# Half of the first modulation's weights streamed by TensorE, another order of the opening, and chunk 1's first products taken row tile by row tile

## The chip, the cores and the metric

The kernel runs on one core of a Trainium2 chip. The metric is device time of one execution in microseconds. The kernel before was run three times: median 1368.39 us, 1365.68 to 1372.27. A further execution was recorded by the hardware profiler; all rows of the profile are from that one.

The engines are named as in the profile: PE is TensorE (products), PEld its weight loads, DVE is VectorE, ACT is ScalarE, POOL is GpSimd, SP is SyncE, which issues nearly all loads and stores here.

## The reference

Two layers of a transformer trunk on 1024 tokens of width 1024 (batch 1), in float32. Each layer is

```
mod = silu(c) @ w_ada[layer] + b_ada[layer]          # 1024 -> 3 x 1024: shift, scale, gate
h   = rmsnorm(x, g_pre) * (1 + scale) + shift
y   = mixer(h)                                       # h @ w_in, attention of two kinds, gates, @ w_out
x   = x + gate * rmsnorm(y, g_post)
```

Layer 0's mixer is latent attention beside sliding-window attention; layer 1's is differential attention beside forgetting attention. The case is about the very beginning: layer 0's shift and scale (2048 numbers, each a sum over 1024 rows of `w_ada`), the first `h`, and the first columns of `h @ w_in`.

## The kernel before, in words

**Layout.** Everything is held transposed: a tile has 128 features as partitions and C = 512 tokens as columns. The 1024 tokens are two chunks, 0 and 1; the 1024 features are eight row tiles, kc 0 to 7. `x` is 8 tiles per chunk, 256 KB each.

**Products.** A value is held as a high part and a low part, both in the fp32r type, so that a product of a weight tile and a tile of h is three matmuls of 128x512 (`kstep`, lines 127, 128, 130): high x high, high x low, low x high. Eight row tiles are accumulated in one PSUM bank: 24 matmuls for 128 output features of one chunk. A weight is loaded in two halves of 256 KB through the ring `wr` (3 buffers, `weight`, line 107), and split: ACT copies the high part (line 91), POOL subtracts (line 92).

**The modulation.** `ada` takes four tiles of 128 outputs at a time, a *group*. The weights of a group come as eight tiles of 128x512 (rows kc, 512 outputs), `raw` with ten buffers. ACT scales the first by silu(c) (line 286), DVE multiplies and adds the other seven to the sum `acc` (line 283). Then the 128 partitions of `acc` have to be added up: `mod_tiles` does that with one plain f32 matmul of each 128 columns against a column of ones (line 295), and a few small DVE instructions add the bias and form shift and scale (lines 304, 306). Layer 0's shift and scale are four such groups; group q holds what the row tiles 2q and 2q + 1 of h need.

**The rms.** `squares` squares the eight tiles of x on ACT (line 190) and adds them on DVE (line 194). `rstd` sums over partitions with f32 matmuls (line 204), takes the inverse root with a dozen small DVE instructions, and spreads the result with f32 matmuls (line 219); ACT copies it out of PSUM (line 367).

**A tile of h.** `pre_norm`: DVE multiplies x by scale and rms (line 326). For even kc ACT makes the high part (line 332) and DVE the low one (line 333); for odd kc ACT adds the shift (line 329) and makes the high part (line 91), POOL the low one (line 92).

**The opening.** `run` walks through a string, `PLAN`, one letter a step: `x` and `y` load x of chunk 0 and chunk 1; `r` and `s` compute their rms; `A` is a modulation group; `W` loads and splits a weight and takes a PSUM bank; `n` makes tiles of h of chunk 0, as many as there are groups for; `m` makes two of chunk 1; `P` issues the products that have become possible with chunk 0, weight by weight. There are five weights (K = 5): three tiles of the latent query, two of the latent key and value. Their banks are the two halves of the pair S, then pj, o, pj. After the plan the five banks are emptied (`keep`: ACT lines 672 and 673, DVE line 674), and chunk 1's products follow, one weight after the other with all eight row tiles, in banks taken in the same order. Then `setup2`, and the remaining first-stage weights with the other modulation groups behind them (`ada_behind`, `project`).

**What sets the order.** The code is written in that order, but a list scheduler places the instructions: it takes what is ready by its own estimate of times, in the order of the code as priority, with `high_priority(offset=60)` moving the folds and the tiles of h ahead. So a loader, or a product whose bank is still full, is passed by a later one. The result is one fixed order for each engine; on the chip each engine takes its own in order and waits where something isn't there yet. SP likewise issues its loads in one order and waits where a buffer isn't free.

Of the kernel before, what the change touches and what calls it, by code (L numbers as in the profile page):

```python
# [14 lines left out]
AF = mybir.ActivationFunctionType  # L15
ALU = mybir.AluOpType
# [6 lines left out]
C = 512  # L23
# [4 lines left out]

PLAN = "xAWWrnWyPAWnAPWnsAPnnmmmmP"


class Trunk:
# [253 lines left out]
        with self.tc.high_priority(offset=60):  # L288
            self.mod_tiles(l, tiles, a)

    def mod_tiles(self, l, tiles, a):
        nc = self.nc
        p = self.psum("pt")
        for j in range(len(tiles)):
            nc.tensor.matmul(p[:, j:j + 1], a[:, j * 128:j * 128 + 128], self.ones, start=True, stop=True)
        runs = []
        for j, t in enumerate(tiles):
            if runs and t == runs[-1][1] + runs[-1][2] and t % 8:
                runs[-1][2] += 1
            else:  # L300
                runs.append([j, t, 1])
        for j, t, n in runs:
            m = self.mod[l][:, t:t + n]
            nc.vector.tensor_tensor(out=m, in0=p[:, j:j + n], in1=self.v_bada[:, l * 24 + t:l * 24 + t + n], op=ALU.add)
            if t // 8 == 1:
                nc.vector.scalar_tensor_tensor(out=m, in0=m, scalar=1.0, in1=self.v_gpre[:, l * 8 + t - 8:l * 8 + t - 8 + n],
                                               op0=ALU.add, op1=ALU.mult)
            elif t // 8 == 2:
                g = self.v_gpost[:, l * 8 + t - 16:l * 8 + t - 16 + n]
                nc.vector.scalar_tensor_tensor(out=m, in0=m, scalar=0.5, in1=g, op0=ALU.mult, op1=ALU.mult)  # L310
# [851 lines left out]
    def run(self):  # L1162
# [3 lines left out]
        h = [[], []]  # L1166
# [3 lines left out]
        with self.tc.tile_pool(name="early", bufs=1) as early:  # L1170
# [13 lines left out]
            for step in PLAN:  # L1184
# [4 lines left out]
                    rs[ch] = self.copied(self.rstd(self.squares(xs[ch]), 1024))  # L1189
                elif step == "A":  # L1190
                    tiles = [2 * q, 2 * q + 1, 8 + 2 * q, 9 + 2 * q]
                    self.drain(self.ada(0, lambda kc: I["wadaa"][q, kc], tiles,
                                        self.t("acc", [128, C], bufs=2, pool=early), raw))
                    q += 1
                elif step == "W":
                    j = first[len(ws)]
                    ws.append(self.weight(j[0], 8, 128, early if len(ws) > 1 else None))
                    banks.append(self.bank(True) if len(banks) < 5 else self.psum("o"))
                    done.append(0)
                elif step == "n":  # L1200
                    with self.tc.high_priority(offset=60):
                        for kc in range(len(h[0]), min(8, 2 * q)):
                            h[0].append(self.pre_norm(0, kc, xs[0][kc], rs[0]))
                elif step == "m":
                    for kc in range(len(h[1]), min(8, len(h[1]) + 2, len(h[0]))):
                        h[1].append(self.pre_norm(0, kc, xs[1][kc], rs[1]))
                else:
                    for n, (w, p) in enumerate(zip(ws, banks)):
                        for kk in range(done[n], len(h[0])):
                            self.kstep(p, w, kk, h[0][kk], kk == 0, kk == 7)  # L1210
                        done[n] = len(h[0])
# [4 lines left out]
            late = [first[n][3][0][3](0, banks[n]) for n in range(K)]  # L1216
            for kc in range(len(h[1]), 8):
                h[1].append(self.pre_norm(0, kc, xs[1][kc], rs[1]))
            for n in range(K):
                p = self.bank(True)  # L1220
                for k in range(8):
                    self.kstep(p, ws[n], k, h[1][k], k == 0, k == 7)
                late.append(first[n][3][0][3](1, p))
            for f in late:
                if f:
                    f()
# [215 lines left out]
```

## Time and profile before

| | |
|---|---|
| median of 3 runs | 1368.39 us (1365.68 to 1372.27) |
| the profiled execution's own time | 1368.67 us |
| its span, first to last instruction | 1366.9 us |
| mean granted TensorE clock | 0.987 |
| PE busy | 1269.7 us, 93% |
| DVE busy | 912.3 us, 67% |
| ACT busy | 734.4 us, 54% |
| POOL busy | 352.5 us, 26% |
| first product of a weight with h | at 29.12 us |
| last product of the first five weights | starts at 108.78 us |

How to read the rows: a row of a group is line, engine, operation, output<-input by the program's names, partitions x elements of both, count | busy us, mean ns of one | idle time of the engine just before them and what ended it. A row of a timeline is start, duration, engine, line, operation, count, and in brackets the idle time before it with its releaser. The record of a matmul has a modelled end and overlaps the next; the distance from start to start is its pace. "raw<-in_wadaa_dram" are the loads of the first modulation's weights; `wx` are weights held in the opening's own memory, `wh` and `wl` those in the common one.

### The profile page before, as it was taken

The page shows a single profiled execution, that of the slowest core. Times are in us where ns is not written, and L with a number is a line of the kernel's source. Part 1 is how long each engine was busy: PE and PEld are TensorE (multiplying, and loading weights), DVE is VectorE, ACT ScalarE, POOL GpSimd, SP SyncE. Part 2 cuts the span into 40 slices and gives each one's busy share as a digit, 9 for nine tenths or more (in the row PEclk, how much of TensorE's full clock was granted, in tenths as well). Part 3 has the DMA queues.
Part 4 walks back from the last instruction along what each step waited for, and adds up shares of the span by engine and source line. Part 5 has one row for each costly group of instructions (what it writes and reads, how often), then busy time and mean ns, then how long its engine had stood idle before and what let it go on. Part 6 is the DMA issues. An engine that isn't in the chain of part 4 may idle for free.

```text
span 1366.9 us, 20727 instructions
## 1 busy us (share of the span) xinstructions
PE 1269.7 (93%) x6876; PEld 1055.4 (77%) x6876; DVE 912.3 (67%) x2058; ACT 734.4 (54%) x1515; POOL 352.5 (26%) x324
## 2 busy tenths in 40 slices
PE   2899999999999999999979999999999999999996
PEld 1678778888777777777757878787888888887896
DVE  6855757777668785787866776667646564656475
ACT  4253226555558577765545554447545455556542
POOL 2243421331233215300003322321222212233400
PEclk9999999999999999999999999999999999999998
DMA  8606685555354444373533222212112121233283
GB/s 284 249 19 210 194 277 189 170 161 178 109 158 138 156 124 138 103 231 123 176 92 104 70 59 66 49 56 76 52 38 78 54 78 55 85 117 103 78 270 121
DMA packets 103723, 173.85 MB, mean 127 GB/s; under 512 B 16304, under 2 KB 25520, under 8 KB 103616
## 3 DMA queue, kind: packets, MB, share of 16 engines
q1 hardware_dynamic: 99104, 169.91, 38.9%
q10 hardware_dynamic: 4512, 2.62, 0.6%
q8 instruction: 54, 0.88, 0.3%
q14 instruction: 53, 0.43, 0.1%
HBM read 129.36 MB, written 31.72 MB: 118 GB/s over the span
## 4 chain that ended last, share of the span: by engine, by line
PE 42%; DVE 12%; ACT 6%; issue 5%; DMA 5%; POOL 1%; SPq 1%; POOLq 0%; DVEq 0%; ACTq 0%
PE pj L127 8%; PE pj L128 8%; PE pj L130 8%; PE S L441 6%; PE pt L501 3%; PE o L511 2%; DVE pt_l L92 1%; DVE p L463 1%; DMA wr<-in_wout_dram 1%; PE o L510 1%; ACT wh L91 1%; PE S L127 1%; PE S L130 1%; PE S L128 1%; DMA t<-wd 1%
## 5 line engine op out<-in xcount | busy, mean ns | idle before, releaser
L127 PE MATMUL pj<-h,wh 128*128 128x512 f32 (+1 forms) x816 | 338.9, 416 | 1.5 <-ACT wh L91 1.5
L128 PE MATMUL pj<-h,wh 128*128 128x512 f32 (+1 forms) x816 | 322.2, 395 | 0.0
L130 PE MATMUL pj<-h,wl 128*128 128x512 f32 (+1 forms) x800 | 316.0, 395 | 2.2 <-DVE wl L92 2.2
L92 POOL TENSOR_TENSOR wl<-wr,wh 128x512 fp32r<-128x512 f32 x126 | 166.4, 1330 | 461.5 <-ACT wh L91 428.9
L466 ACT ACTIVATE p<-p,sm 128x128 f32<-128x128 f32 (+3 forms) x192 | 148.8, 775 | 146.8 <-DVE sm L463 143.0
L92 DVE TENSOR_TENSOR pt_l<-pt,pt_h 128x512 fp32r<-128x512 f32 (+1 forms) x232 | 146.9, 635 | 99.4 <-ACT pt_h L91 97.5
L441 PE MATMUL S<-qk,qk 96*128 96x512 f32 (+5 forms) x720 | 175.3, 344 | 20.6 <-DVE sm L463 11.4
L130 PEld LDWEIGHTS pj<-h,wl 128*128 128x128 f32 x800 | 151.0, 189 | 35.0 <-DVE wl L92 3.8
L91 ACT ACTIVATE pt_h<-pt 128x512 fp32r<-128x512 f32 (+1 forms) x232 | 127.6, 552 | 89.3 <-PE pt L501 87.5
L127 PEld LDWEIGHTS pj<-h,wh 128*128 128x128 f32 (+1 forms) x816 | 153.9, 189 | 20.3 <-ACT wh L91 2.3
L441 PEld LDWEIGHTS S<-qk,qk 128*128 128x128 f32 (+1 forms) x720 | 120.2, 188 | 63.2 <-DVE sm L463 25.5
L128 PEld LDWEIGHTS pj<-h,wh 128*128 128x128 f32 (+1 forms) x816 | 154.4, 189 | 17.1 <-DVE h L92 0.2
L91 ACT ACTIVATE wh<-wr 128x512 fp32r<-128x512 f32 x165 | 100.9, 622 | 115.4 <-PE S L128 38.6
L501 PE MATMUL pt<-ident,p 128*128 128x128 f32 x840 | 134.3, 274 | 3.1 <-DVE p L945 3.1
L501 PEld LDWEIGHTS pt<-ident,p 128*128 128x128 f32 x840 | 101.5, 140 | 26.1 <-DVE p L945 4.4
L463 DVE CUSTOM_DVE_ANT_0 p<-S,mask 128x640 f32<-128x640 f32 (+7 forms) x128 | 96.0, 750 | 35.0 <-PE S L441 34.1
L510 PE MATMUL o<-pt_h,v 128*128 128x256 f32 (+1 forms) x408 | 106.3, 279 | 2.1 <-ACT pt_h L91 1.7
L511 PE MATMUL o<-pt_l,v 128*128 128x256 f32 (+1 forms) x408 | 102.3, 285 | 5.6 <-DVE pt_l L92 5.3
L348 POOL TENSOR_TENSOR t<-t,rs 128x512 f32<-128x512 f32 x26 | 36.8, 1414 | 229.0 <-DMA t<-t 147.4
L511 PEld LDWEIGHTS o<-pt_l,v 128*128 128x128 f32 x408 | 77.2, 189 | 16.6 <-DVE pt_l L92 11.2
L510 PEld LDWEIGHTS o<-pt_h,v 128*128 128x128 f32 x408 | 77.0, 189 | 11.2 <-ACT pt_h L91 4.8
L127 PE MATMUL S<-h,wh 128*128 128x512 f32 (+1 forms) x144 | 57.5, 399 | 3.9 <-ACT h L332 2.7
(317 smaller groups left out, 2288.6 us busy)
## 6 DMA issues: line engine op xcount, KB each, us to landing
wr<-in_wod_dram SPq DMA_DIRECT2D x80, 256.0 KB
wr<-in_wout_dram SPq DMA_DIRECT2D x68, 256.0 KB
ad<-in_wadab_dram SPq DMA_DIRECT2D x41, 256.0 KB
wr<-in_wev_dram SPq DMA_DIRECT2D x38, 256.0 KB
raw<-in_wadaa_dram SPq DMA_DIRECT2D x32, 256.0 KB
ogd<-t SPq DMA_DIRECT2D x32, 256.0 KB
t<-t SPq DMA_DIRECT2D x106, 64.0 KB
t<-rd SPq DMA_DIRECT2D x48, 128.0 KB
```

Of the source, the lines that this page charges most:

```text
L91: nc.scalar.activation(hi, src, AF.Copy)
L92: (lo_eng or nc.vector).tensor_tensor(out=lo, in0=src, in1=hi.bitcast(F32), op=ALU.subtract)
L127: nc.tensor.matmul(p, w[0][:, k, :m], h[0], start=first, stop=False)
L128: nc.tensor.matmul(p, w[0][:, k, :m], h[1], start=False, stop=last and w[1] is None)
L130: nc.tensor.matmul(p, w[1][:, k, :m], h[0], start=False, stop=last)
L348: nc.gpsimd.tensor_tensor(out=s, in0=s, in1=self.rs[:, cs], op=ALU.mult)
L441: nc.tensor.matmul(dst, a, k[:, s], start=(n == 0), stop=n == len(q) - 1)
L463: nc.vector.tensor_tensor_reduce(out=P[:, s], in0=S[:, s], in1=a, scale=-scale, scalar=init, op0=ALU.add, op1=ALU.min, accum_out=nm)
L466: nc.scalar.activation(P[:, :n], P[:, :n], AF.Exp, bias=nm, scale=-1.0, accum_out=l)
L501: nc.tensor.transpose(pt[:, n * 128:n * 128 + 128], b, self.ident)
L510: nc.tensor.matmul(o[:, qcols], w, hi[:, cols], start=start, stop=False)
L511: nc.tensor.matmul(o[:, qcols], w, lo[:, cols], start=False, stop=stop)
```

## The change

Three things.

1. A new `ada_first` takes the place of `ada` in the opening. Of a group's eight weight tiles the first four go to PE: a plain f32 matmul with the column kc of silu(c) as weight (one column) and the weight tile as the moving operand (512 columns), accumulated in a one-partition slice of an `o` bank. ACT copies that row of 512 to memory. The other four go on as before: ACT scales kc 4, DVE adds kc 5, 6 and 7. `mod_tiles` then folds both: for each 128 outputs one matmul of the row (one partition) against a one, and one of `acc` against the column of ones, into the same PSUM column.

2. The plan is another: the rms of chunk 0 directly behind its load, the groups one step ahead of the tiles of h of the group before, the second and third weight behind the third group, chunk 1's load behind the fourth. An `n` makes exactly two tiles.

3. Chunk 1's products of the five weights are issued in two sets, three weights and then two; in a set each row tile of h goes through all weights before the next.

```diff
-PLAN = "xAWWrnWyPAWnAPWnsAPnnmmmmP"
+
+PLAN = "xrAWAnAWWPnAyWPnsWPnmmmmP"
...
-    def mod_tiles(self, l, tiles, a):
+    def ada_first(self, l, w, tiles, a, row, raw):
+
+        nc = self.nc
+        p = self.psum("o")[:1]
+        for kc in range(8):
+            r = raw()
+            nc.sync.dma_start(r, w(kc))
+            if kc < 4:
+                nc.tensor.matmul(p, self.sc[:, kc:kc + 1], r, start=kc == 0, stop=kc == 3)
+                if kc == 3:
+                    nc.scalar.activation(row, p, AF.Copy)
+            elif kc > 4:
+                nc.vector.scalar_tensor_tensor(out=a, in0=r, scalar=self.sc[:, kc:kc + 1], in1=a,
+                                               op0=ALU.mult, op1=ALU.add)
+            else:
+                nc.scalar.activation(a, r, AF.Copy, scale=self.sc[:, kc:kc + 1])
+        with self.tc.high_priority(offset=60):
+            self.mod_tiles(l, tiles, a, row)
+
+    def mod_tiles(self, l, tiles, a, row=None):
         nc = self.nc
         p = self.psum("pt")
         for j in range(len(tiles)):
-            nc.tensor.matmul(p[:, j:j + 1], a[:, j * 128:j * 128 + 128], self.ones, start=True, stop=True)
+            s = slice(j * 128, j * 128 + 128)
+            if row is not None:
+                nc.tensor.matmul(p[:, j:j + 1], row[:, s], self.ones[:1], start=True, stop=False)
+            nc.tensor.matmul(p[:, j:j + 1], a[:, s], self.ones, start=row is None, stop=True)
...
                 elif step == "A":
                     tiles = [2 * q, 2 * q + 1, 8 + 2 * q, 9 + 2 * q]
-                    self.drain(self.ada(0, lambda kc: I["wadaa"][q, kc], tiles,
-                                        self.t("acc", [128, C], bufs=2, pool=early), raw))
+                    self.ada_first(0, lambda kc: I["wadaa"][q, kc], tiles, self.t("acc", [128, C], bufs=2, pool=early),
+                                   self.t("row", [1, C], bufs=2, pool=early), raw)
                     q += 1
...
-                        for kc in range(len(h[0]), min(8, 2 * q)):
+                        for kc in range(len(h[0]), len(h[0]) + 2):
                             h[0].append(self.pre_norm(0, kc, xs[0][kc], rs[0]))
...
-            for n in range(K):
-                p = self.bank(True)
+            for group in ((0, 1, 2), (3, 4)):
+                banks = {n: self.bank(True) for n in group}
                 for k in range(8):
-                    self.kstep(p, ws[n], k, h[1][k], k == 0, k == 7)
-                late.append(first[n][3][0][3](1, p))
+                    for n in group:
+                        self.kstep(banks[n], ws[n], k, h[1][k], k == 0, k == 7)
+                for n in group:
+                    late.append(first[n][3][0][3](1, banks[n]))
```

## The prediction

> **What bounds the kernel now.** I read the page first: TensorE (PE) is busy for 93% of the span, so time is mostly to be had where it isn't. The row of 40 slices puts the largest hole at the start, which is also where the whole change lies. So I cut the start into stretches (columns: stretch and its length, then busy us with counts of PE, weight loads, DVE, ACT and POOL, the granted clock, DMA share, GB/s).
>
> ```profile
> 0.00:10.40 10.40, 0.00 (x0) 0.00 (x0) 3.20 (x10) 4.83 (x8) 0.20 (x4) 1.00 0.74 242
> 10.40:29.10 18.70, 5.62 (x24) 5.26 (x24) 12.30 (x28) 7.91 (x13) 6.42 (x5) 1.00 0.81 278
> 29.10:56.00 26.90, 18.69 (x56) 13.86 (x56) 24.44 (x28) 11.71 (x19) 11.42 (x8) 0.87 0.78 278
> 56.00:85.30 29.30, 26.51 (x124) 20.09 (x124) 24.07 (x44) 14.82 (x25) 9.09 (x6) 1.00 0.28 105
> 85.30:109.00 23.70, 23.70 (x102) 19.21 (x103) 5.26 (x7) 9.54 (x18) 11.82 (x10) 1.00 0.13 39
> 109.00:160.00 51.00, 50.17 (x258) 41.90 (x257) 34.66 (x88) 12.99 (x25) 19.52 (x16) 1.00 0.69 216
> ```
>
> From 85.3 to 109.0 PE is full: 102 products in 23.7 us, 0.232 us each. Before that VectorE (DVE) is the full one, 24.4 of 26.9 us and 24.1 of 29.3. The timeline gives the chain.
>
> ```profile
> 13.33 5.47 DVE L283 SCALAR_TENSOR_TENSOR acc<-raw,sc,acc 128x512 f32<-128x512 f32 x7
> 18.86 1.86 PE L295 MATMUL pt<-ones,acc 128*128 128x1 f32 x8 [18.86 <-DVE acc L283]
> 24.74 2.04 PE L219 MATMUL pt<-ident,sm 128*128 128x128 f32 x8 [2.32 <-issue]
> 29.12 0.80 PE L127 MATMUL S<-h,wh 128*128 128x512 f32 x1 [2.33 <-ACT h L332]
> 33.29 0.80 PE L128 MATMUL S<-h,wh 128*128 128x512 f32 x1 [2.95 <-DVE h L333]
> 69.58 2.08 DVE L326 SCALAR_TENSOR_TENSOR h<-h,mod,t 128x512 f32<-128x512 f32 x3
> 83.79 0.78 DVE L333 SCALAR_TENSOR_TENSOR h<-h,mod,h 128x512 fp32r<-128x512 f32 x1 [1.09 <-ACT h L332]
> 85.29 0.50 PE L127 MATMUL S<-h,wh 128*128 128x512 f32 x1 [0.47 <-DVE qk L674]
> 108.78 0.40 PE L130 MATMUL pj<-h,wx 128*128 128x512 f32 x1
> ```
>
> DVE sums a modulation group (L283), PE folds it, DVE makes tiles of h; products of the first five weights begin at 29.1 and at full density at 85.3. The last DVE piece of h ends at 84.6, and chunk 1's products end at 109.0. That end is the mark I work with: past it PE is busy 50.2 of 51 us (last row of the table), and the diff touches nothing there, so I let everything behind 109 move with it.
>
> **Part 1: half the modulation to PE.** These are DVE's groups of the first 110 us.
>
> ```profile
> L283 DVE SCALAR_TENSOR_TENSOR acc<-raw,sc,acc 128x512 f32<-128x512 f32 x28 | 25.6, 916 | 0.5
> L326 DVE SCALAR_TENSOR_TENSOR h<-h,mod,t 128x512 f32<-128x512 f32 x15 | 12.6, 881 | 2.2 <-ACT t L367 2.1
> ```
>
> Of seven multiply-adds a group keeps three (kc 5 to 7; kc 4 is ACT's scaled copy, as kc 0 was). Removed: 16 x 0.916 = 14.7 us of DVE. DVE is nearly full from 13.3 to 84.6, so the last tile of h could come at 84.6 - 14.7 = 69.9. Behind it, in the new order, stand 9 + 48 products, 57 x 0.232 = 13.2 us: DVE alone would allow an end at 83. PE's own work decides whether that is reached.
>
> Added to PE are 16 matmuls in plain f32, one weight column and 512 moving columns. No such instruction is in the trace. What is there:
>
> ```profile
> L295 PE MATMUL pt<-ones,acc 128*128 128x1 f32 x32 | 5.7, 298 | 23.8 <-DVE acc L283 23.8
> 113.59 1.05 PE L219 MATMUL pt<-ident,sm 128*128 128x128 f32 x8
> 114.48 0.95 PE L204 MATMUL pt<-ones,t 128*128 128x1 f32 x8
> 33.89 0.63 PE L130 MATMUL S<-h,wl 128*128 128x512 f32 x1
> 34.31 0.63 PE L127 MATMUL S<-h,wh 128*128 128x512 f32 x1
> 39.01 0.42 PE L127 MATMUL pj<-h,wx 128*128 128x512 f32 x1
> 39.27 0.39 PE L128 MATMUL pj<-h,wx 128*128 128x512 f32 x1
> ```
>
> The code folds 16 tiles with 16 matmuls and the trace has 32 records: a plain f32 matmul is two records. Lower bound for 512 columns: two records at the pace of the fp32r products, 2 x 0.232 = 0.46 us. Upper bound: L219 takes 1.05/8 = 0.13 us per record of 128 columns; four times that, twice, is 1.05 us. I take 0.9, near the upper end, because L219 is the same number type and the fp32r products are not. 16 x 0.9 = 14.4 us (7.4 to 16.8). [...]
>
> The pace holds only at the full clock. The last four rows show it: products start 0.42 us apart at 34, and 0.26 apart at 39, 5.7 us after the run of products began at 33.3. The first run of the new kernel pays this too: some 5.6 us at half pace lose 2.8 us.
>
> Folding doubles: a group's 4 matmuls become 8 (the row's, K = 1, too), 64 records in all against 32, at L204's 0.95/8 = 0.12 us: 7.6 us. (No K = 1 load is in the trace; L204's record is my upper end, and zero for the added half the lower, 3.8 us.) The two rstd stay: 2 x (0.95 + 1.05) = 4.0 us. ACT gains four copies of a 1x512 row out of PSUM.
>
> ```profile
> L367 ACT ACTIVATE t<-pt 128x512 f32<-128x512 f32 x2 | 1.2, 598 | 12.1 <-PE pt L219 12.1
> L673 ACT ACTIVATE qk<-S,vecs 128x512 fp32r<-128x512 f32 x4 | 2.7, 677 | 0.0
> L672 ACT ACTIVATE t<-S 128x512 f32<-128x512 f32 x4 | 2.3, 584 | 0.8 <-PE S L130 0.8
> L674 DVE SCALAR_TENSOR_TENSOR qk<-S,vecs,qk 128x512 fp32r<-128x512 f32 x4 | 3.0, 745 | 11.1 <-ACT qk L673 11.1
> ```
>
> The full-height copy takes 0.60 us, so 0 to 0.6 each and 2.4 us of an ACT that is busy 11.7 of 26.9 us; each adds up to 0.6 us ahead of a fold. The folds run under other products except the first, which nothing covers.
>
> **Part 2: the order.** All loads are issued by SP, in one order.
>
> ```profile
> GB/s 0 160 293 293 325 389 398 348 396 376 231 15 210 222 281 259 359 397 399 389 386 384 384 389 377 240 121 20 164 150 210 118 387 365 396 379 212 6 0 0
> raw<-in_wadaa_dram SPq DMA_DIRECT2D x32, 256.0 KB
> SPq L281 <- DVE acc L283: 10.7, 8, 3.7
> 40.84 13.77 SPq L281 DMA_DIRECT2D raw<-in_wadaa_dram  x8
> ```
>
> The first is the rate of the first 70 us in 40 slices. At its best it is 385 to 399 GB/s, and it falls to 20 where SP waits for raw buffers (10 of them), which DVE was freeing: 10.7 us in all, and the last group's 8 issues take from 40.8 to 54.6. With x, y (8 each), 32 raws and 10 weight halves, 58 x 0.262 = 15.2 MB at 390 GB/s take 39 us. So even with everything ahead of it the last group lands by about 42 instead of 57. Its tiles of h are then ready near 42 + 2 (stream left over) + 2 (fold) + 3 (tile) = 49. PE's other work without those 30 products and chunk 1 lasts until 57 or later, so loads don't bound either. A raw that PE frees late holds SP, and behind it y and the last two weights: that is in the second rival.
>
> First tile of h: the first window's 242 GB/s give 2.5 MB by 10.4, which is x, the constants and the first raw; PE can stream from there. The rstd no longer waits behind seven multiply-adds on DVE, nor the fold. Four streams at half pace, 4 x 1.8, put the row copy at about 17.5; fold 2 us, DVE's four small ones under 1, h 2 to 3: near 23 to 24, not 29.1. The gap is filled by the second group's stream.
>
> **Part 3: chunk 1 row tile by row tile.** The same 120 products; three banks must be empty before their first product, not one. Emptying a bank is 0.58 + 0.68 on ACT and 0.75 on DVE; three need 3 x 1.26 + 0.75 = 4.5 us, and the last two banks of chunk 0 cover 12 x 0.232 = 2.8: up to 1.7 us shows. The gain of the order, that a late tile of h holds up 9 products and not a whole weight, is worth under 1.5 us in the trace of before (PE full after 85.3). The next weights get a freed buffer 48 x 0.232 = 11.1 us ahead of the end, enough for a split of two halves. I book the part at 1 us lost.
>
> **The sum.** PE from 10.4: products 240 x 0.232 = 55.7, streams 14.4, folds 7.6, rstd 4.0, together 81.7; cold start 2.8; waits 3.6 (1 for part 3, about 2.6 around the first folds and the first weights' splits). End: 10.4 + 81.7 + 2.8 + 3.6 = 98.5 instead of 109.0, 10.5 us less. The profiled execution took 1368.67 us (span 1366.9 and 1.8 around it), the median of the runs is 0.3 less: 1358.2, and 1358 is my number. Its own range is 1353 to 1362: waits from 0 to 8, folds 3.8 to 7.6.
>
> **The rivals.** (a) *The stream is cheaper*, two passes at 0.46: 7 us less on PE, and DVE (83) and loads still don't bind: end 91, 1350. For it: fp32r does 512 columns in 0.232. Against: L219.
>
> (b) *PE's fixed order waits.* A stream that waits for its raw holds every product behind it, and PE, not DVE, now frees raws. PE idles 6 us more: end 104.5, 1364. For it: SP's waits above, and PE's idle 23.8 us before L295. Against: raws land 0.67 us apart, faster than PE takes them at 0.9.
>
> (c) *The drain shows in full*: the three banks' emptying sits behind tiles of h on DVE, 4.5 us: end 102, 1362. For it: before, PE waited at 85.3 for just this L674. Against: PE is now the late one.
>
> (d) *Slower: the clock stays half through the streams.* One-column matmuls may not raise it. A record is then 0.22 us (1.86 for eight at 18.86) and a stream twice as long: a group costs 4 x 0.9 + 16 x 0.12 = 5.5 us more. The forecast has 10.5 + 2.8 us to lose, so it decides from the third group on; with three groups and the first rstd (2 us) it is 18.5 - 13.3 = 5 us slower: 1374. For it: after 18.86 PE did 3.7 and 2.0 us of such small work, and the products at 33.3 were still slow. Against: 5.6 us of products were needed as well, and gaps of over 2 us lay between. [...]
>
> **The numbers.** Forecast 0.50, (a) 0.12, (b) 0.18, (c) 0.10, (d) 0.10. A measurement can tell about 0.5%, 6.8 us: faster means under 1361.5. Nearly all of the forecast, (a) and a third of (c) give 0.64; (b), the rest of (c) and the forecast's edge 0.26; (d) 0.10. The range 1348 to 1370 leaves out (d) and the far edge of (a).
>
> **What would show it.** Right: 32 records of 128x512 f32 with one weight column near 0.45 us apart once warm; L283 x12; the first product of h near 24; the last of chunk 1 near 98; PE, not DVE, full from 25 on. Wrong: such records 0.23 or 0.9 us apart after 20 us, PE idle over 8 us between 25 and 98 with a raw or a bank named as releaser, a first product later than 27, or an end of the opening that moves while the total doesn't.

## The result, and the profile after

| | before | after |
|---|---|---|
| median | 1368.72 us (1365.68 to 1372.27, 4 runs) | 1386.49 us (1385.74 to 1392.32, 4 runs) |
| ratio, 95% interval | | 1.0146 [1.0126, 1.0165] |
| the profiled execution | 1368.67 us, span 1366.9 | 1392.32 us, span 1390.3 |
| mean granted clock | 0.987 | 0.979 |
| last product of the first five weights starts | 108.78 | 123.08 |

The change makes the kernel slower: 1.5% by the ratio, 17.8 us or 1.3% by the two medians. The forecast had 0.8% faster, and the time lies outside its range of 1348 to 1370. The profiled execution of after is the slowest of its four. In after.py the stream is L300, the copy of the row L302, DVE's multiply-add L304, the folds L317 (row) and L318 (`acc`), products L128, L129 and L131, rms sums L205.

The stretches of the first 160 us, cut where the prediction cut before (busy us and counts of PE, weight loads, DVE, ACT, POOL; granted clock; DMA share; GB/s):

```profile
10.40:29.10 18.70, 15.80 (x45) 6.93 (x46) 9.24 (x25) 6.48 (x11) 2.48 (x2) 0.91 0.77 274
29.10:56.00 26.90, 25.74 (x80) 12.42 (x79) 13.52 (x21) 9.35 (x16) 7.55 (x6) 0.81 0.71 233
56.00:85.30 29.30, 22.37 (x92) 17.62 (x91) 15.76 (x26) 9.95 (x18) 9.10 (x6) 0.83 0.43 155
85.30:109.00 23.70, 22.02 (x96) 17.61 (x95) 13.26 (x17) 13.06 (x22) 9.28 (x7) 1.00 0.00 0
109.00:160.00 51.00, 50.20 (x258) 42.01 (x256) 28.75 (x77) 17.31 (x32) 21.50 (x18) 1.00 0.59 187
```

DVE has been relieved as foretold: 13.5 and 15.8 us where it had 24.4 and 24.1. PE is the busy engine from the first raw on, 25.7 of 26.9 us. Yet it gets less done in that time: up to 85 the granted clock is 0.81 to 0.83, and at 109 it still works on the opening.

PE's timeline shows at which pace it works (start, duration of the row, count, idle time before it):

```profile
13.04 1.87 PE L300 MATMUL o<-raw,sc 128*1 128x512 f32 x2 [13.04 <-DMA raw<-in_wadaa_dram]
14.84 1.87 PE L205 MATMUL pt<-ones,t 128*128 128x1 f32 x8
16.64 5.10 PE L300 MATMUL o<-raw,sc 128*1 128x512 f32 x6
21.67 0.49 PE L220 MATMUL pt<-ident,sm 128*128 128x128 f32 x2
22.42 0.38 PE L317 MATMUL pt<-ones,row 1*128 1x1 f32 x2 [0.26 <-ACT row L302]
...
24.59 0.38 PE L318 MATMUL pt<-ones,acc 128*128 128x1 f32 x2
24.83 1.63 PE L220 MATMUL pt<-ident,sm 128*128 128x128 f32 x6
26.39 4.51 PE L300 MATMUL o<-raw,sc 128*1 128x512 f32 x8
30.82 0.50 PE L128 MATMUL S<-h,wh 128*128 128x512 f32 x1
36.04 6.50 PE L300 MATMUL o<-raw,sc 128*1 128x512 f32 x8
51.51 2.73 PE L300 MATMUL o<-raw,sc 128*1 128x512 f32 x6
54.17 0.50 PE L129 MATMUL S<-h,wh 128*128 128x512 f32 x1
75.20 1.84 PE L205 MATMUL pt<-ones,t 128*128 128x1 f32 x8 [4.64 <-DVE t L195]
97.93 0.50 PE L128 MATMUL S<-h,wh 128*128 128x512 f32 x1 [1.68 <-DVE qk L697]
123.08 0.40 PE L131 MATMUL pj<-h,wx 128*128 128x512 f32 x1
```

The six stream records at 51.51 reach to the next row at 54.17: 2.66 us, 0.44 each, two to a matmul: 0.89 us, as booked. Those at 16.64 reach to 21.67: 0.84 each. From start to start and without waits the four groups' streams take 6.8, 4.4, 6.5 and 3.6 us. The windows around the change of pace show when the clock falls (columns as above):

```profile
22.00:25.00 3.00, 2.74 (x19) 2.48 (x18) 0.00 (x0) 1.41 (x3) 2.04 (x2) 0.97 0.93 326
25.00:28.00 3.00, 3.00 (x8) 1.37 (x9) 1.30 (x5) 0.69 (x2) 0.45 (x1) 0.50 0.04 15
34.00:36.00 2.00, 2.00 (x12) 1.93 (x11) 0.00 (x0) 0.00 (x0) 0.00 (x0) 0.77 0.91 255
36.00:38.00 2.00, 2.00 (x4) 0.36 (x5) 1.78 (x5) 0.61 (x1) 0.00 (x0) 0.50 1.00 374
```

In both places the fall comes in a run of folds or at its end (22.4 to 24.8, and 33.5 to 36), with a gap of 0.26 us before the one and 0.48 us before the other and none in them; what comes next then begins at half the pace. The folds from 43.2 to 45.8, behind a gap of 0.68 us, end in the same way (0.83 from 44 to 46, 0.50 from 46 to 48). Those from 57.3 to 59.3 don't (1.00 from 57 to 60), and the fourth fall, at 72.6 (0.94 from 70 to 73, 0.50 from 73 to 76), lies in the wait of 4.64 us, with no fold near. Streams do bring the clock up again: 26.39 starts at 0.50, from 28 to 30 it is 0.94, and the products at 31 are at full pace, 0.23 to 0.24 us apart.

What PE waited for in the first 124 us (us in total, times, longest):

```profile
PE o L300 <- DMA raw<-in_wadaa_dram: 13.0, 1, 13.0
PE pt L205 <- DVE t L195: 4.6, 1, 4.6
PE S L128 <- ACT h L355: 1.8, 1, 1.8
PE S L128 <- DVE qk L697: 1.7, 1, 1.7
PE pt L317 <- ACT row L302: 0.9, 2, 0.7
```

**The account.** I took PE's timeline from its first matmul to the end of chunk 1's products of the first five weights ("the opening's end") and added up the distances from start to start by kind of work, with the idle time before a row counted apart as a wait. "Half" is what of the products' time comes from records 0.38 to 0.46 us apart, over 0.232.

| us | first PE | stream | folds | rms | products | of it half | waits | end |
|---|---|---|---|---|---|---|---|---|
| forecast | 10.4 | 14.4 | 7.6 | 4.0 | 58.5 | 2.8 | 3.6 | 98.5 |
| before | 18.9 | 0 | 5.1 | 5.6 | 63.9 | 5.4 | 15.6 | 109.0 |
| after | 13.0 | 21.4 | 10.2 | 6.4 | 62.4 | 4.2 | 10.0 | 123.3 |

Against before, PE got 21.4 + 5.1 + 0.8 - 1.5 = 25.8 us more to do, while its waits and its late start gave back only 5.6 + 5.9 = 11.5: 14.3 later. The total is 17.8 later by the medians and 23.6 in the profiled pair.

### The profile page after: what moved, and what is told of

Same layout as the page of the kernel before. It is cut to its first block, busy times and chain, and to the rows that moved or that the text cites. A ratio compares the mean times of both kernels' runs of the same rounds, so it can differ in the third digit from the quotient of the medians.

```text
span 1390.3 us, 20829 instructions
## 1 busy us (share of the span) xinstructions
PE 1298.6 (93%) x6940; PEld 1065.2 (77%) x6940; DVE 904.9 (65%) x2042; ACT 735.0 (53%) x1519; POOL 350.8 (25%) x324
## 4 chain that ended last, share of the span: by engine, by line
PE 42%; DVE 11%; ACT 6%; DMA 5%; issue 5%; POOL 1%; SPq 0%; POOLq 0%; DVEq 0%; ACTq 0%
PE pj L128 8%; PE pj L129 8%; PE pj L131 8%; PE S L464 6%; PE pt L524 3%; DMA wr<-in_wout_dram 2%; PE o L534 2%; PE o L533 1%; DMA t<-wd 1%; DVE p L486 1%; DVE pt_l L93 1%; ACT wh L92 1%; DMA wr<-in_wod_dram 1%; PE S L128 1%; PE S L131 1%
## 5 line engine op out<-in xcount | busy, mean ns | idle before, releaser
L128 PE MATMUL pj<-h,wh 128*128 128x512 f32 (+1 forms) x816 | 339.5, 416 | 1.4 <-ACT wh L92 1.3
L129 PE MATMUL pj<-h,wh 128*128 128x512 f32 (+1 forms) x816 | 322.8, 396 | 0.0
L131 PE MATMUL pj<-h,wl 128*128 128x512 f32 (+1 forms) x800 | 316.5, 396 | 2.3 <-DVE wl L93 2.3
L131 PEld LDWEIGHTS pj<-h,wl 128*128 128x128 f32 x800 | 151.4, 189 | 35.2 <-DVE wl L93 3.8
L128 PEld LDWEIGHTS pj<-h,wh 128*128 128x128 f32 (+1 forms) x816 | 154.2, 189 | 20.1 <-ACT wh L92 2.2
L129 PEld LDWEIGHTS pj<-h,wh 128*128 128x128 f32 (+1 forms) x816 | 154.8, 190 | 17.0 <-DVE h L93 0.2
L534 PEld LDWEIGHTS o<-pt_l,v 128*128 128x128 f32 x408 | 77.6, 190 | 16.7 <-DVE pt_l L93 11.1
L128 PE MATMUL S<-h,wh 128*128 128x512 f32 (+1 forms) x144 | 56.5, 392 | 5.6 <-ACT h L355 1.8
```

What stands on the lines that cost most here:

```text
L128: nc.tensor.matmul(p, w[0][:, k, :m], h[0], start=first, stop=False)
L129: nc.tensor.matmul(p, w[0][:, k, :m], h[1], start=False, stop=last and w[1] is None)
L131: nc.tensor.matmul(p, w[1][:, k, :m], h[0], start=False, stop=last)
L534: nc.tensor.matmul(o[:, qcols], w, lo[:, cols], start=False, stop=stop)
```

## The experiments

The theories, by the letters of the expectations. P: PE's added time lies on the path and shows. O: chunk 1's load comes too late. C1: a stream with one weight column counts as idle for the clock. C2: the doubled folds cost more than their count, since runs of them let the clock fall. Q: SP is held at the ring of weights, and the raws behind it. F: PE's fixed order puts chunk 1's rms sum ahead of products that are ready. R: the end hangs on that rms sum. S: what counts is PE time added for each us taken from DVE; in the two runs with the early sum S stands for another thing, that PE's added work alone sets the end. W: what PE is spared is waited out elsewhere in its fixed order.

All results; each ratio is to the runs of before on the same chip. "End" is the opening's end in one execution, the profiled one. It is the slowest of its kernel's in some rows (after, e1, e4, e13) and the fastest in others (e7, e10, e11, e14, e15); how far an end differs from execution to execution is not known.

| run | median us | ratio [95%] | end |
|---|---|---|---|
| e1_order | 1375.97 | 1.0064 [1.0040, 1.0088] | 115.0 |
| e2_stream | 1382.50 | 1.0122 [1.0092, 1.0151] | 120.5 |
| e3_rows | 1371.12 | 1.0029 [1.0012, 1.0046] | 108.5 |
| e4_y_early | 1384.25 | 1.0124 [1.0090, 1.0158] | 121.0 |
| e5_wide | 1384.99 | 1.0138 [1.0105, 1.0170] | 122.5 |
| e6_fold | 1375.25 | 1.0070 [1.0042, 1.0099] | 113.7 |
| e7_half | 1385.71 | 1.0146 [1.0114, 1.0179] | 124.7 |
| e8_two | 1377.64 | 1.0100 [1.0066, 1.0133] | 116.0 |
| e9_wr4 | 1387.83 | 1.0133 [1.0103, 1.0163] | 125.4 |
| e10_s_late | 1380.88 | 1.0097 [1.0072, 1.0121] | 115.9 |
| e11_fold_s_late | 1378.41 | 1.0078 [1.0059, 1.0096] | 114.0 |
| e12_all | 1376.08 | 1.0058 [1.0038, 1.0078] | 112.8 |
| e13_s_early | 1385.29 | 1.0100 [1.0064, 1.0137] | 118.7 |
| e14_s_early_fold | 1374.60 | 1.0041 [1.0016, 1.0065] | 113.6 |
| e15_s_early_fold_half | 1370.69 | 1.0005 [0.9989, 1.0020] | 110.2 |
| e16_s_early_dve | 1374.25 | 1.0040 [1.0020, 1.0059] | 115.1 |
| e17_last2 | 1376.15 | 1.0058 [1.0034, 1.0082] | 110.5 |
| e18_last3 | 1375.62 | 1.0064 [1.0045, 1.0083] | 118.3 |

### One part alone

The order alone: before with the new plan and the new rule of `n`.

```diff
-PLAN = "xAWWrnWyPAWnAPWnsAPnnmmmmP"
+PLAN = "xrAWAnAWWPnAyWPnsWPnmmmmP"
-                        for kc in range(len(h[0]), min(8, 2 * q)):
+                        for kc in range(len(h[0]), len(h[0]) + 2):
```

> The new plan string alone, with the whole modulation on DVE and chunk 1 weight by weight. Theory O (order): chunk 1's load behind the fourth group makes its rms and so its tiles of h late; then this alone is 10 to 20 us slower than before (1378 to 1388). Theory P (PE's added work: the streams and the doubled folds at half clock, with everything behind them in PE's fixed order): the order alone costs nothing, 1364 to 1372.

The stream alone: after with the old plan, the old rule and chunk 1 weight by weight.

```diff
-PLAN = "xrAWAnAWWPnAyWPnsWPnmmmmP"
+PLAN = "xAWWrnWyPAWnAPWnsAPnnmmmmP"
...
-            for group in ((0, 1, 2), (3, 4)):
+            for n in range(K):
...
```

> The stream on PE alone, in the old plan and with chunk 1 weight by weight. Theory P: 8 to 18 us slower than before (1376 to 1386), streams of 20 us and folds of 10 us on PE. Theory O: the streams relieve DVE and fill idle time of PE, 1358 to 1368.

Chunk 1 by row tiles alone: before with the new loop.

```diff
-            for n in range(K):
+            for group in ((0, 1, 2), (3, 4)):
...
```

> Chunk 1's products row tile by row tile alone. Both theories: within 2 us of before (1366 to 1371); the first weight's buffer comes free later, which should be hidden.

Measured: the order alone costs 0.6%, the stream alone 1.2%, the row tiles 0.3%. The order alone lies between O and P (9 us over before); the stream alone is where P has it. In the account the order alone, with DVE still summing, has waits of 22.9 instead of 15.6, though PE starts at 13.3 instead of 18.9. The stream alone gives PE 20.5 for streams and 11.1 for folds, and the waits fall by 2.1. So the stream with its folds is the main loss: it puts the end 11.5 us later in the old order, and 8.3 later in the new one (115.0 to 123.3, with the row tiles). The row tiles move the end by -0.6 only; the 4 us by which their median is above before (ten runs) do not show in the opening of the profiled execution, the second fastest of the ten.

### Loads, and the streams' own effect on the clock

Chunk 1's load ahead of the second group, and an extra buffer so that the second weight's loads don't wait in the ring (`row` with one buffer to make room):

```diff
# e4_y_early
-PLAN = "xrAWAnAWWPnAyWPnsWPnmmmmP"
+PLAN = "xrAWyAnAWWPnAWPnsWPnmmmmP"
# e9_wr4
-            raw = self.t("wr", [128, 4, 128])[:, :s.stop - k, :m]
+            raw = (more() if more and k else self.t("wr", [128, 4, 128]))[:, :s.stop - k, :m]
...
```

> The changed kernel with chunk 1's load moved up: behind the first group instead of the fourth. Theory O: the rms of chunk 1 is done some 20 us earlier, the idle time of PE near 70 to 75 and the half clock behind it go, 12 to 20 us faster than the changed kernel (1366 to 1374). Theory P: within 4 us of the changed kernel (1383 to 1390).

> The changed kernel with a fourth buffer for the halves of the second weight, so that SP's loads of the second and third weight no longer wait for a split (the row copies have one buffer instead of two, to make room). Theory Q (the opening waits for loads: SP stands at the weight ring from 34.7 to 45.1 with six raws of the fourth group and chunk 1's load behind it): these raws are issued before 38, and the end of the opening comes 6 to 10 us earlier, 1375 to 1381. Theory C2 (folds and half clock): within 3 us of the changed kernel, 1383 to 1390.

Neither gains what O and Q foretold (12 to 20 us, and 6 to 10). SP's timeline of after and of the run with the extra buffer, the issues of the last group's raws (start, time from the first issue to the last, count):

```profile
45.47 2.79 SPq L298 DMA_DIRECT2D raw<-in_wadaa_dram  x6
```

```profile
34.43 6.35 SPq L298 DMA_DIRECT2D raw<-in_wadaa_dram  x8
```

With the extra buffer the last six raws of the last group are issued some 7 to 10 us sooner, and the end is at 125.4 instead of 123.3: Q falls. With chunk 1's load moved up its rms sum on PE still stands at 72.5 (75.2 in after), so the load isn't what makes that sum late, and O falls.

The weight column repeated over 128 columns, so that the weight is as wide as that of a product:

```diff
# e5_wide
-        p = self.psum("o")[:1]
+        p = self.psum("o")
-                nc.tensor.matmul(p, self.sc[:, kc:kc + 1], r, start=kc == 0, stop=kc == 3)
+                nc.tensor.matmul(p, self.sc[:, kc:kc + 1].to_broadcast([128, 128]), r, start=kc == 0, stop=kc == 3)
-                    nc.scalar.activation(row, p, AF.Copy)
+                    nc.scalar.activation(row, p[:1], AF.Copy)
```

> The changed kernel with the stream's weight column broadcast to 128 columns, so that the whole array works; the first partition of the result is used as before. Theory C1 (the clock falls because a one-column matmul counts as idle): streams now run near 0.43 us a record throughout, 6 to 10 us less of stream, 1376 to 1381. Theory C2 (streams do raise the clock, and the runs of folds let it fall): streams keep the same mixture of 0.43 and 0.85 us, within 4 us of the changed kernel (1382 to 1390).

The stream costs 18.0 instead of 21.4, folds and waits a little more, the end is 0.8 earlier and the total doesn't differ. Its first streams are at half pace too:

```profile
15.21 4.77 PE L300 MATMUL o<-raw,sc 128*128 128x512 f32 x6
24.89 5.83 PE L300 MATMUL o<-raw,sc 128*128 128x512 f32 x8
34.45 3.68 PE L300 MATMUL o<-raw,sc 128*128 128x512 f32 x8
```

C1 falls, since the 6 to 10 us that it foretold do not come: with one column and with 128 the clock goes up and down alike (0.91 and 0.81 from 10.4 to 29.1 and from 29.1 to 56 in after, 0.82 and 0.87 here).

### Less streaming

Half the columns streamed (256 of 512; half of the stream's sums are left out, and the half that is there is copied twice to fill the row), and two of eight tiles streamed instead of four:

```diff
# e7_half
-                nc.tensor.matmul(p, self.sc[:, kc:kc + 1], r, start=kc == 0, stop=kc == 3)
+                nc.tensor.matmul(p[:, :256], self.sc[:, kc:kc + 1], r[:, :256], start=kc == 0, stop=kc == 3)
...
# e8_two
-            if kc < 4:
+            if kc < 2:
...
```

> The changed kernel with each stream matmul over 256 of the 512 columns; half of the stream's sums is left out, and ACT copies the half row twice (0.4 us more on ACT, four times). Loads, buffers, folds and orders stay. Theory P (PE's added time lies on the path of the opening): the stream goes from 21 to 11 us and the end of the opening and the total by 8 to 11: 1375 to 1379. Theory W: the streams' time is waited out elsewhere, within 3 us of the changed kernel.

> The changed kernel with two of a group's eight weight tiles on PE and five multiply-adds on DVE. Theory P: half the stream goes, DVE gets 7 us back of the 14.7 it was spared, and PE sets the end: 6 to 10 us faster than the changed kernel (1376 to 1381). If DVE sets the end, no gain or slower (1386 and up).

With half the columns the streams take 12.6, 8.8 us less, and the end comes no sooner (+1.4): folds 14.3 (+4.1), products 66.7 (+4.3), waits 13.4 (+3.4). What the streams no longer cost, slower folds and products and the waits took. In its simple form P falls here, and W's figure holds. With two tiles streamed the end is 7.3 earlier and the total 9 us less than after, which is P's figure, and 1% above before.

### The fold

The row goes into `acc` on DVE before the fold, so that a fold is four matmuls again and ACT copies nothing:

```diff
# e6_fold
-                if kc == 3:
-                    nc.scalar.activation(row, p, AF.Copy)
...
+        nc.vector.tensor_tensor(out=a[:1], in0=a[:1], in1=p, op=ALU.add)
         with self.tc.high_priority(offset=60):
-            self.mod_tiles(l, tiles, a, row)
+            self.mod_tiles(l, tiles, a)
```

> The changed kernel with the row out of PSUM added to the first partition of acc by DVE (four instructions), so that ACT copies no row and a group is folded by 4 matmuls as in the kernel before. Theory C2: folds go from 10 us to 5, and the clock no longer falls behind each: 6 to 12 us faster than the changed kernel (1374 to 1380). Theory W (what costs is waiting in PE's fixed order): within 3 us of it (1383 to 1390).

This is the largest single gain: the end at 113.7, 9.6 earlier, the total 1375.25, 11 us less than after. Folds fall from 10.2 to 4.3, streams from 21.4 to 17.0. A fold in its timeline:

```profile
21.77 0.95 PE L317 MATMUL pt<-ones,acc 128*128 128x1 f32 x8
```

A whole fold is 0.95 us where after takes from 22.42 to 24.8. C2's figure holds, in the fold's own price and in that of the streams behind it: -5.9 and -4.4; the rest comes to +0.6 (products +0.5, waits +2.5, rms -1.7, first PE -0.7). The granted clock reads 1.00 up to 29.1 here, past the first fold, and the second one, at 31.03, still takes 1.05 us; the third, at 40.34, takes 1.87, behind a wait of 3.15 us. The edit also takes ACT's copy of the row out of the way; the two are not told apart.

### Chunk 1's rms sum

In after, chunk 1's squares are added up late, as DVE's timeline shows; ACT's row from the first tile of h is put below it.

```profile
59.97 1.42 DVE L349 SCALAR_TENSOR_TENSOR h<-h,mod,t 128x512 f32<-128x512 f32 x2
64.34 10.71 DVE L195 TENSOR_TENSOR t<-t,t 128x512 f32<-128x512 f32 x7 [0.81 <-ACT t L191]
```

```profile
27.91 0.72 ACT L355 ACTIVATE h<-h,mod 128x512 fp32r<-128x512 f32 x1 [0.82 <-DVE h L349]
```

Seven additions take from 64.3 to 75.1, and PE, whose order has the sum ahead of further products, waits 4.64 us (the row at 75.20). The third row is of use further below. The sum moved behind the last tiles of h, alone, with the cheap fold, and with the fold and two extra weight buffers:

```diff
# e10_s_late; also e11_fold_s_late (with e6's edit), e12_all (with e6's and two of e9's buffers)
-PLAN = "xrAWAnAWWPnAyWPnsWPnmmmmP"
+PLAN = "xrAWAnAWWPnAyWPnWPnsmmmmP"
```

> The changed kernel with the rms of chunk 1 put behind the next products of chunk 0 in the plan (sWP becomes WPnWPns). Theory F (in PE's fixed order the sum for chunk 1's rms stands ahead of products that are ready, PE waits 4.6 us for it and falls to half clock for 7 more): both go, 5 to 9 us faster than the changed kernel, 1378 to 1382. If these waits are only moved, within 3 us of it.

> Both the row added by DVE (4 matmuls a fold) and the late rms of chunk 1. If the two add up, 5 to 8 us under the first alone: 1367 to 1371. If the same wait was behind both, 1373 to 1377.

> Row added by DVE, late rms of chunk 1, and two more buffers for the weights' second halves. If theories C2, F and Q each hold and add up: 1358 to 1366, faster than the kernel before. If Q is void: as the run before it, 1367 to 1371.

The sum moved early, with chunk 1's load behind the first group; and with that plan the cheap fold, the cheap fold with half the stream's columns (half of its sums left out), and before with all on DVE:

```diff
# e13_s_early; also e14 (with e6's edit), e15 (with e6's and e7's), e16 (before with this plan and the new n)
-PLAN = "xrAWAnAWWPnAyWPnsWPnmmmmP"
+PLAN = "xrAyWAnAsWWPnAWPnWPnmmmmP"
```

> The changed kernel with chunk 1's load behind the first group and its rms ahead of the first products (xrAyWAnAsWWP...). Theory R (the end of the opening is pinned to the sum for chunk 1's rms on PE, some 175 products or 45 to 48 us ahead of it, and that sum is late because ACT's and DVE's fixed orders put the squares behind the tiles that wait for the fourth group's fold): the sum comes before 50, and the end drops from 123 to what PE's work adds up to, 111 to 116; total 1374 to 1380. Rival S (PE's added work alone sets the end): within 3 us of the changed kernel, 1383 to 1390.

> The same with the row added by DVE, so that a group is folded by 4 matmuls. Theory R: PE's sum is 6 us lower and the clock falls less often, end 103 to 108, total 1362 to 1370. Rival S: 1372 to 1376, as with the fold alone.

> The kernel of the run before with each stream over 256 of 512 columns; half of the stream's sums is left out. With the rms early, theory R lets the stream's time count: 5 to 9 us under the run before. If within 2 us of it, the stream's length is still not on the path.

> The same order (chunk 1's load and rms early) with the whole modulation on DVE and chunk 1 weight by weight: the kernel before with another plan string. Theory R: the late rms was the cost of the new order, so the end comes back from 115 to 105 to 110, total 1362 to 1370. Rival: the order costs through the weights' late loads, 1373 to 1378 as with the new order alone.

| us | rms sum at | products behind it | end minus sum |
|---|---|---|---|
| after | 75.2 | 176 | 48.1 |
| e7_half | 77.7 | 173 | 47.0 |
| e9_wr4 | 77.9 | 176 | 47.5 |
| e10_s_late | 74.1 | 150 | 41.8 |
| e12_all | 71.0 | 149 | 41.8 |
| e13_s_early | 46.4 | 234 | 72.3 |
| e15_s_early_fold_half | 47.7 | 234 | 62.5 |

In after and in the two runs below it the end is the rms sum plus 47 to 48 us of products behind it, and half the stream or earlier raws didn't bring that sum sooner; so far R fits. F holds: with the sum late, 26 more products go ahead of it and the end is 7.4 earlier, the total 5.6 less. It doesn't add up with the fold (114.0 against 113.7 without it): the totals of the fold with the late sum, 1378.41, and with the extra buffers too, 1376.08, lie outside both figures that were foretold for each.

What R foretold for an early sum did not come. The sum came before 50, but the end only 4.6 sooner and the total 1.2: 118.7 and 1385.29, where R had 111 to 116 and 1374 to 1380. With the cheap fold, and with everything on DVE, R had an end of 103 to 110 and 1362 to 1370 in total; measured were 113.6 and 115.1, 1374.60 and 1374.25. All three totals are the rivals'. So the late sum was one limit with another close behind it. Freed of the sum, PE has no hole left from 56 on:

```profile
56.00:85.30 29.30, 29.30 (x119) 21.00 (x118) 16.66 (x25) 15.35 (x25) 16.85 (x11) 0.93 0.35 117
85.30:118.70 33.40, 33.40 (x146) 26.88 (x144) 6.01 (x8) 11.64 (x21) 11.54 (x9) 1.00 0.10 28
```

That is the early sum's run from 56 to its end: 62.7 of 62.7 us busy. In this form a part of P comes back: half the columns (11.4 us of streams instead of 20.4) now take 3.4 off the end and 3.9 off the total, where 5 to 9 were foretold. Not even that is faster than before; and the same plan without any stream is no better than with the stream and the cheap fold (1374.25 and 1374.60).

### Is it the price, or the idea?

Before as it was, but the last two (or three) weight tiles of a group go straight into the fold: 128 columns of the tile as weight, one column of silu(c) as moving operand, into the same PSUM column. No stream, no row, no copy, no other order.

```diff
# e17_last2 (e18_last3: 3)
...
+            if last and kc >= 8 - last:
+                held.append((r, kc))
...
+            s = slice(j * 128, j * 128 + 128)
+            nc.tensor.matmul(p[:, j:j + 1], a[:, s], self.ones, start=True, stop=not held)
+            for r, kc in held:
+                nc.tensor.matmul(p[:, j:j + 1], r[:, s], self.sc[:, kc:kc + 1], start=False, stop=kc == 7)
```

> The kernel before (its plan, its order of chunk 1), with one edit: the last two weight tiles of each opening group (kc 6 and 7) are no longer multiplied and added on DVE; they go straight into the fold, 128 columns of the weight tile as weight and one column of silu(c) as the moving operand, accumulated in the same PSUM column as the sum of the other six. No row of PSUM, no copy of it. PE gets 4 groups x 16 more records; by the folds of the changed kernel (0.12 to 0.155 us a record) that is 7.7 to 9.9 us, DVE loses 8 x 0.916 = 7.3 us. Theory S (what decides is how much PE time is added for one us taken from DVE: the changed kernel pays 21.4 + 5.1 for 14.7, 1.8 to one; this pays 1.0 to 1.4 to one and the holes of before, 15.6 us, take it): opening's end at 103 to 109, total 0 to 6 us under the kernel before. Theory C2 (a run of one-column records lets the clock fall, and it falls whenever such a run exceeds 2.4 us): folds of 24 records run 2.9 to 3.7 us each, the products behind lose 2 to 3 us each time: end 110 to 115, total 3 to 8 us over the kernel before.

> As the run with the last two tiles, with the last three (kc 5, 6 and 7). PE gets 4 x 24 more records, 11.5 to 14.9 us; DVE loses 12 x 0.916 = 11.0 us. Theory S: the holes of before are nearly used up, end 102 to 110, total -6 to +2 us against the kernel before. Theory C2: folds of 32 records run 3.8 to 5 us each at a clock that falls in every one: end 113 to 120, total 5 to 12 us over the kernel before.

Both came out near C2's figures and not S's, one total a shade above C2's bound: ends of 110.5 and 118.3, totals 8.2 and 7.6 us over before. The second fold of the run with two tiles, and what stands behind it; below it the granted clock of that place (columns as in the windows above):

```profile
38.51 0.28 PE L299 MATMUL pt<-ones,acc 128*128 128x1 f32 x2
38.65 0.58 PE L301 MATMUL pt<-sc,raw 128*128 128x1 f32 x4
...
40.44 0.39 PE L299 MATMUL pt<-ones,acc 128*128 128x1 f32 x2
40.69 0.99 PE L301 MATMUL pt<-sc,raw 128*128 128x1 f32 x4
41.54 0.78 PE L127 MATMUL o<-h,wx 128*128 128x512 f32 x1
42.12 0.63 PE L128 MATMUL o<-h,wx 128*128 128x512 f32 x1
```

```profile
40.00:42.00 2.00, 2.00 (x13) 2.00 (x13) 1.80 (x2) 0.34 (x1) 2.00 (x2) 0.66 0.90 331
42.00:44.00 2.00, 2.00 (x5) 1.01 (x4) 1.88 (x2) 0.00 (x0) 1.05 (x1) 0.50 0.76 244
```

At 38.65 four records take 0.45 us, at 40.69 0.85: some 2 us into the run of one-column matmuls, without a gap before it or in it, the clock halves (0.66 from 40 to 42, 0.50 from 42 to 44). All 24 are full-height here, so the one row of after's folds isn't needed for it. Not every run does it, though, so C2's "whenever" is too strong: in the run with the stream alone, folds and a rms sum behind them take from 18.09 to 21.46, 3.4 us of one-column records without an idle time in its timeline, and the two stream records at 21.46 still take 1.02 us together, where at half clock two take 1.87. Folds cost 13.5 and 20.6 us in the two kernels against 5.1, for 7.3 and 11.0 us less on DVE by its old pace: 1.15 and 1.4 to one, where after pays 26.5 for 14.7, 1.8 to one. The price is part of it, then, but not all. The run with the row added on DVE pays about 1.1 to one (streams 17.0 and folds 0.8 less than before's, for 14.7), and its waits fall by 3.1 (15.6 to 12.5); with two tiles in the fold they fall by 5.6 (to 10.0).

None of the kernels is faster than before.

## Why the prediction was wrong

**What bounded the kernel** was read right: DVE held the tiles of h, and it was relieved (12 multiply-adds, 10.0 us, where there were 28 of 25.6). What failed is the step called *the sum*: it put all of the new work on PE at the prices of full clock, behind one cold start of 2.8 us, and left 3.6 us of waits where 10.0 were measured. Two of its own signs of being wrong showed: the first product came at 30.82, later than 27, and the stream records at 36.04 were still 0.81 us apart in the mean.

```profile
L304 DVE SCALAR_TENSOR_TENSOR acc<-raw,sc,acc 128x512 f32<-128x512 f32 x12 | 10.0, 834 | 5.5 <-ACT acc L307 5.3
```

Term by term, against 98.5: the first stream at 13.0, not 10.4 (+2.6); streams 21.4 for 14.4 (+7.0); products with the half clock 62.4 for 58.5 (+3.9); folds 10.2 for 7.6 (+2.6); rms 6.4 for 4.0 (+2.4); waits 10.0 for 3.6 (+6.4). Together, but for rounding, the whole distance from 98.5 to 123.3. The table books the forecast's cold start under products, though the prediction lays it on the new kernel's first run, which is of streams; booked there, streams are 4.2 over and products 6.7.

- *The stream's price.* 0.9 us a matmul was right at full clock (0.44 a record; 3.6 us for the fourth group's four). 0.89 us is 3.8 times the 0.232 of a product. The bounds of 7.4 to 16.8 held no half clock for any but the first group. Over 3.6 us a group the first took 3.2 more, which the cold start covers but for 0.4; the half clock came back in the second and the third, 0.8 and 2.9 more.
- *Rival (d)*, the half clock, had the sign and 1374 us, 12 short. Its cause, that matmuls with one weight column don't raise the clock, is wrong: the rows at 26.39 and 30.82 and the streams that run alone from 36.04 until the clock is back at 41.9 (0.52 from 40 to 42, 1.00 from 42 to 44) show that they do. It fell in the folds, whose matmuls have one moving column. In after the three falls up to 46 us had no gap over 0.7 us ahead of them, and the one at 40.6 in the run with two tiles in the fold had none.
- *Rival (b)*, PE's fixed order, had 6 us more of idle; the waits are 6.4 over the forecast's. The forecast treated it as another case; it came on top. (Of the 23.8 us of idle time that the prediction quotes for it, 18.9 lie before PE's first matmul.) The largest wait is on the rms sum (4.64), which the text had not named. PE's order also put the second group's four streams (26.39 to 30.8) ahead of the first product, whose tile of h ACT had finished at 28.6 (27.91 and 0.72); "near 24" for that product failed there and at the late first raw.
- *Rival (c)*, the drain: 1.68 us at 97.93, as bounded (1.7). Part 3's "1 us lost" did not show with the row tiles alone, which put the end 0.6 us sooner.
- *Rival (a)*, with 0.46 us for the two records of a stream matmul, falls with 0.44 for each. The lower edge of the forecast's own range is mis-added, too: no waits and folds of 3.8 us give 1351, not 1353.
- *"I let everything behind 109 move with it."* It moved by more. From the first transposition of attention weights (`pt<-ident,p`) at 203.38 (before) and 218.44 (after) to the 262nd record of the same kind at 457.98 and 479.82, work that the diff doesn't touch, after takes 6.8 us longer. The order of PE's, DVE's and ACT's instructions from 203.38 and 218.44 on is the same in both, so another schedule is not the reason. The fourth of five equal slices of that stretch in before and in after:

```profile
356.10:407.00 50.90, 47.86 (x280) 40.64 (x280) 35.58 (x62) 26.72 (x58) 15.06 (x14) 1.00 0.47 145
```

```profile
375.20:427.50 52.30, 47.17 (x268) 40.03 (x267) 33.88 (x61) 25.06 (x54) 14.50 (x13) 0.97 0.45 138
```

The waits of PE in the whole stretch are 4.0 us more (13.3 against 9.3), and the clock is at 0.97 to 0.99 in three fifths of it. From the marker at 203 to the last spread of an rms (1357.60 and 1380.99) after loses 8.3 us in all, 6.8 of them in waits of PE; the run with two tiles in the fold loses 6.9, and the one with the early sum and the cheap fold gives 3.7 back. These are single executions, after's the slowest and the last one's the fastest of theirs. So the opening's end tells a profiled execution's time to some 8 us only, and why the later work runs better or worse behind another opening stays open.

**The deeper fault** is that the sum was never made for before. By the same account before has 15.6 us of waits and, against the forecast's 10.4, 8.5 us of late start: 24.1 in all. The change adds 16.9 us to PE even at the forecast's prices (streams 14.4, and folds of 7.6 in place of 5.1). To end 10.5 us sooner nevertheless, the forecast had to take back 20.5 of the 24.1, all of the late start and 12.0 of the waits. After took back 11.5. The lowest waits of the eighteen experiments are 7.4 us.

## What to carry to other kernels

Before work goes to an engine that is full elsewhere in the same stretch, add up its idle time in that stretch and ask which of it can be filled at all; here less than half was (11.5 of 24.1 us). Price moved work at the clock that it will run at, and ask what it does to the clock of the work behind it: many matmuls with one moving column in a row can cost twice, once themselves and once in what follows (with half as many, folds took 5.9 us less here, and streams 4.4). A small sum over partitions is better merged into the tile that is folded anyway (one DVE addition of one row, 11 us less in total) than folded on its own.

## What the runs showed of the hardware

The granted clock fell to half in runs of one-column f32 matmuls of 2 to 3 us, or right behind them, without a gap in them: near 40.6 in the run with two tiles (0.66 from 40 to 42, 0.50 from 42 to 44), near 24.8 and 35.1 in after (0.97 from 22 to 25, 0.50 from 25 to 28; 0.77 from 34 to 36, 0.50 from 36 to 38). It fell in a wait, too: near 72.6 in after (0.94 from 70 to 73, 0.50 from 73 to 76), where PE waited 4.64 us. Other runs of one-column matmuls ended at full pace: in after the one from 57.33 to 59.33, in the stream alone the one from 18.09 to 21.46. What sets the ones apart from the others was not shown.

The clock came back with streams of 512 columns. With one weight column, in after, from 38 to 44 (columns as above):

```profile
38.00:40.00 2.00, 2.00 (x3) 0.25 (x2) 0.77 (x2) 1.97 (x4) 0.49 (x1) 0.50 0.54 207
40.00:42.00 2.00, 2.00 (x4) 0.25 (x2) 1.88 (x2) 0.05 (x1) 0.78 (x1) 0.52 0.00 0
42.00:44.00 2.00, 1.32 (x8) 0.76 (x6) 0.87 (x2) 1.43 (x3) 0.24 (x1) 1.00 0.01 4
```

With 128, in the run with the column repeated, the eight records at 24.89 take 0.66 us each in the mean (to 30.16), and the products behind them, at 30.79 and 31.02, are 0.23 apart; the eight at 34.45 take 0.46 each.

A plain f32 matmul of 512 columns is two records, 0.44 us each at full clock and 0.84 at half. In after's folds, where matmuls over one row and over 128 rows alternate, each takes 0.31 us at full clock (2.17 us from 22.42 to 24.59 for seven), the one over one row no less; where all are over 128 rows, the run with two tiles has 0.22 (two records of the four in 0.45). What the alternation has to do with it was not tried. The granted clock of the profile can't be read for the first streams: it is 1.00 from 16.6 to 21.4 in after, while the streams at 16.64 go at half pace (0.84 us a record).
